# A two-layer diffusion trunk: the last down sweep's weights summed by accumulating DMAs, another order of the down sweeps, and a new plan of the second attention

## The chip, the cores and the metric

The kernel runs on one core of one Trainium2 chip. That core has five engines with instruction streams of their own: TensorE (PE in the profile, with the weight loads listed as PEld), VectorE (DVE), ScalarE (ACT), GpSimd (POOL) and SyncE (SP, which here only issues DMAs). Each executes its stream in order; they wait for one another by semaphores. SBUF is the on-chip memory of 128 partitions, PSUM the memory into which TensorE writes its products.

The metric is the time of one execution on the device in microseconds (us), the median of three runs.

## The reference

A stream of 1024 latent tokens and 256 context tokens, 1024 wide, goes through two layers. Layer 0 mixes tokens by neighbourhood attention, layer 1 by sliding-window attention (radius 128) with 16 query heads over 4 key heads, rotary positions and a sink logit per head. Both layers end with a gated feed-forward part with a convolution of width 3. Context tokens are carried through layer 0 and are only read in layer 1.

```python
for i in range(2):
    sh1, sc1, gt1, sh2, sc2, gt2 = split(silu(c) @ w_mod[i] + b_mod[i])        # the same for the context
    h = rmsnorm(x, g_attn[i]) * (1 + sc1) + sh1
    q, k, v = h @ w_in, q and k normalised per head (rotary in layer 1)
    x = x + gt1 * (attend(q, [k, k_c], [v, v_c]) @ w_out)
    h = rmsnorm(x, g_ffn[i]) * (1 + sc2) + sh2
    u = conv3(h @ w_up) + b;  a, g = halves(u)                                # 2 x 2816 wide
    x = x + gt2 * ((a * silu(g)) @ w_down)
```

Everything is float32 within a tolerance, so the kernel splits each operand of a product into a high and a low part (`whi`/`wlo`, `ghi`/`glo`, `h1hi`/`h1lo`) and runs three matmuls: high by high, high by low, low by high.

## The kernel before

**Stages.** Attention of layer 0, feed-forward of layer 0 (`ffn(0, ...)`), attention of layer 1 (the code that fills the scheduler with `plan_ctx_kv`, `plan_norm`, `plan_sw_qkv` and others, called "the second attention" below), feed-forward of layer 1. Activations lie transposed: 8 blocks `k` of 128 features, and the 1024 tokens in two chunks `c` of 512. The stages that the change touches each have a scheduler `Sched`: operations are declared with an engine, a planned duration, dependencies, a key (rank) and buffers, `run` places them one after the other in planned time, and each engine's instructions are then emitted in that order and stay in it (`InOrder`). `RANKS` holds small corrections of the keys by the number of the operation, one table for each stage. Constants tell a stage what the stage before leaves behind: `LAG` (how long after TensorE each engine is still busy with it), `NREADY` (when the sum of squares for a norm is ready), `LANDED` and `STORED` (when certain transfers are done).

**The down projection.** `a * silu(g)` has 2816 features in 22 blocks, taken as 11 pairs (`NP`). One level of a Strassen-like scheme over token chunks and feature halves makes seven products out of eight. They run in five sweeps over the 11 pairs, `plan_pair(si, i)`; sweeps 0 and 1 make two products each (24 matmuls a pair), sweeps 2, 3 and 4 one (12 matmuls a pair). For each pair SP loads the weights `wraw` and the activations `graw` (from `g_dram`, where the up projection stored them, some as differences made in `block`/`t2`); ACT makes `whi` and `ghi`, DVE makes `wlo` and `glo`, and TensorE adds into four accumulators (`dn`, one of 128 features each) of group a, b, c or d. Some weights are sums: `s3(i)` keeps a difference of two weight blocks in SBUF from sweep 0 on (tiles `s` for the first 8 pairs, `s3lo` for the last 3); sweep 1 replaces it by another combination, and sweeps 3 and 4 each load a weight block and combine it with `s3(i)` on DVE (`wraw<-wraw,s` and `wraw<-wraw,s3lo`) before `whi` and `wlo` can be made.

At the end of a sweep the finished accumulators are added to the residual `xn(c, k)` on DVE (`plan_ev`, in the profile `xn<-dn,modc,xn`), and the results go to `x_dram` (`plan_xd`). In layer 0 the order is 0, 1, 2, 3, 4. Chunk 0 is complete after sweep 2, chunk 1's blocks 0 to 7 after sweep 4, whose accumulators d go into both halves: eight evictions at the end.

**The hand-over to the second attention.** `plan_next` prepares it within the last two sweeps. For chunk 0: sum of squares, reciprocal root (DVE `n1v`, a power on POOL `n1y`, three small DVE steps of a Newton iteration `n1t`, `n1t`, `n1y`, then four DVE copies of a scaled identity `nsum<-idr,n1y`, which TensorE spreads over the partitions as `bc`), then per block a product (`xn<-xn,modc,nsum`) and the split `h1hi`/`h1lo`. For chunk 1 only the squares (ACT `sq`) and their sum (DVE `sums`) are made there. The weights of the context's keys and values (`ckv`) are loaded and split at the end. TensorE then starts the second attention with the context's keys and values (`mm<-whi,h1chi`), goes on with the projections of chunk 0 (`mm<-whi,h1hi`, 24 matmuls of 384 columns for one group of heads and 128 tokens), and needs chunk 1 next: `plan_norm` reduces `sums` (`pt<-invd,sums`), runs the same chain (`n1v`, `n1y`, `S<-idr,n1y`, on TensorE `s<-S,ones`), makes `t<-x,modc,s` on DVE, `h1hi` on ACT and `n1lo` on DVE or POOL. In between, q and k of each 128 tokens are normalised and rotated (`qv`, `qy`, `qn`, `qa`, `qb`, `st`, `klt` on DVE, POOL and ACT) and transposed on TensorE (`pt<-idr,st`, `pt<-idr,klt`).

All of these run through the helper at line 51, so the profile's groups are told apart by tiles, not by lines.

Of the kernel before, what the change touches and what calls it, by code (L numbers as in the profile page):

```python
# [17 lines left out]
P = 128  # L18
D = 1024
KT = 8  # L20
# [18 lines left out]
class InOrder:  # L39
# [7 lines left out]
    def __getattr__(self, name):  # L47
        f = getattr(self.eng, name)

        def call(*a, **k):  # L50
# [25 lines left out]
    ffn0={321: 16.4, 346: 3.3, 364: -15.4, 382: 3.9, 387: 4, 388: -8.1, 389: -5.4, 433: -24.5, 499: 13.3, 502: 17,  # L76
          503: -8.5, 519: 1.9, 548: 28.3, 571: 47.3, 1150: -18.3, 3223: -3.9, 3317: 2.1, 3398: 3.9, 3445: -3.9,
          3455: 9.6, 3469: 6.9, 3609: 20, 3613: 6.8},
    sw={6: -33, 8: -15, 11: 29.2, 14: 18.5, 67: -2.8, 73: -2.8, 74: 57.2, 141: -74.9, 152: 3.4, 162: 17.4, 168:
# [189 lines left out]
def trunk_kernel(ctx, tc, xperm, xtok, xseq, cc, wmod0, wmod, bmod, gnorm, na_wqkv, na_gq, na_gk, na_bias, na_wo,  # L269
# [472 lines left out]
    def plan_norm(sc, l, psa, wk, sums, x, hl, key):  # L742
# [68 lines left out]
        for k in range(KT):  # L811
# [342 lines left out]
    NREADY = 9.2  # L1154
# [279 lines left out]
    def ffn(l, opj, xt1, todo):  # L1434
# [582 lines left out]
        def plan_u(pos, ft, key, C, T):  # L2017
# [55 lines left out]
            sc.op(*LO[512], lambda e: sub(e, YP["t", i][1], V[0][:, :512], YP["t", i][0]), reads=[v, gt + (2,)],  # L2073
# [26 lines left out]
        SWEEPS = (0, 1, 3, 4, 2) if last else (0, 1, 2, 3, 4)  # L2100
# [32 lines left out]
        def plan_pair(si, i):  # L2133
# [10 lines left out]
            def loadg(e):  # L2144
# [6 lines left out]
            sc.op("dma", 1.8 if n > 512 else 1.0, loadw, writes=[I + ("r",)], key=k0 - 14,  # L2151
                  acq=[("raw", I + ("r",), 2 if si == 2 else 3)])
# [7 lines left out]
            elif si == 1:  # L2160
                sc.op(*LO[512], lambda e: sub(e, s3(i), lo_h(), s3(i)), reads=[r_tok], writes=[s_tok], key=k0 - 9, rel=[r_tok])
                src = ((lambda: s3(i), s_tok), (lo_h, r_tok))
            elif si == 2:
                src = ((lo_h, r_tok),)
            else:
                sc.op(*LO[512], lambda e: ENG[e].tensor_tensor(out=lo_h(), in0=lo_h(), in1=s3(i), op=(ALU.subtract, ALU.add)[si - 3]),
                      reads=[s_tok], writes=[r_tok], key=k0 - 9, rel=[r_tok])
                src = ((lo_h, r_tok),)
# [25 lines left out]
            for q in range(nq):  # L2194
                d, starts = prods[q]
                for m in range(4):
                    def mm(e, q=q, m=m, d=d, starts=starts):
# [3 lines left out]
                        for k, (w, g) in enumerate(((0, 0), (0, 1), (1, 0))):  # L2201
# [3 lines left out]
                          writes=[("dn", d, m)], key=k0 + 2.72 * q + (1.36 * m - 2.72 * (i - NP + 2) if si == SWEEPS[-1] and i >= NP - 2 else 0),  # L2205
# [19 lines left out]
        for si in SWEEPS:  # L2225
# [51 lines left out]
    def plan_next(sc, KS, xn, bank, x_tile, plan_sums, plan_bc, plan_t, plan_hilo, u_done, gp, D_):  # L2277
# [50 lines left out]
        for j in range(2):  # L2328
            def load(e, j=j):
# [7 lines left out]
             (lambda k: KS[2] + 5 * (k - 4) if k > 3 else KS[3] - 2 + k, KS[3] + 2, lambda k: KS[3] + 10 + 4 * k),  # L2337
# [7 lines left out]
        for n, k in enumerate(k + 4 * i for k in range(4) for i in range(2)):  # L2345
            ring = ("raw", "sq", "g")[(n % 2 + 1) * (n > 0)]

            def sq(e, k=k, ring=ring):
                if ring == "raw":
                    SQ[k] = sums(e)  # L2350
                elif ring == "sq":
# [4 lines left out]
            sc.op("act", t_act(512), sq, reads=[("xn", 1, k), ("dp",)], writes=[("sq1", k)], key=KS[5], rel=[("xnt", 1, k // 2)],  # L2356
                  acq=[(ring, ("sq1" + ring, k), 1)])

            def add(e, k=k):
                dve.tensor_tensor(out=SQ[0][:, :512], in0=SQ[0][:, :512], in1=SQ[k], op=ALU.add)  # L2360
            if n:
                sc.op("dve", t_dve(512), add, reads=[("sq1", k)], writes=[("sq1", 0)], key=KS[5], rel=[("sq1" + ring, k)])
# [561 lines left out]
```

## Time and profile before

| | us |
|---|---|
| median of three runs (2758.69 to 2758.89) | 2758.88 |
| the profiled execution | 2759.63 |
| its span, first to last instruction | 2757.8 |
| PE busy in the span | 2731.3 |
| DVE, ACT, POOL busy | 2291.1, 1701.8, 418.3 |
| mean granted TensorE clock | 0.999 |

Engine and tile names are those above; `a<-b,c` is an instruction that writes tile a from b and c. In rows of the timeline the first number is the start in us from the span's start, the second the duration of the row's instructions together, `x4` their number, and the bracket at the end the idle time of the engine just before, with what ended it. The times of the profiled execution are used for lengths, the runs for comparisons.

The sweeps of layer 0's down projection lie at about 1423 to 1635 us, the second attention begins there.

### The profile page before, as it was taken

What the parts mean: (1) busy time and instruction counts of PE and PEld (TensorE: products, weight loads), DVE (VectorE), ACT (ScalarE), POOL (GpSimd) and SP (SyncE); (2) the same over time, 40 slices, a digit from 0 to 9 for tenths busy, and PEclk for the clock granted to TensorE, in tenths of its full rate; (3) what the DMA queues carried; (4) which work ended last, traced back from release to release, by engine and by line L of the source; (5) the groups of instructions that cost most, each with busy time, mean ns of one, the idle gap of its engine ahead of it and who ended that gap; (6) DMA issues with size and microseconds to landing.
All of it is one profiled execution on the core that took longest, in us unless ns stands there. A gap on an engine that the chain in (4) does not pass through costs nothing.

```text
span 2757.8 us, 45386 instructions
## 1 busy us (share of the span) xinstructions
PE 2731.3 (99%) x16073; PEld 2431.8 (88%) x16073; DVE 2291.1 (83%) x5005; ACT 1701.8 (62%) x3333; POOL 418.3 (15%) x684
## 2 busy tenths in 40 slices
PE   8999999999999999999999999999999999999999
PEld 7999999999889987788888888999988888888887
DVE  6888878888779678798998698888997989888766
ACT  6877777778556554455554457888874655555443
POOL 1222122223100000000000017546430000000000
PEclk9999999999999999999999999999999999999999
DMA  7222222224745544444476561010254234334745
GB/s 286 80 85 82 73 72 84 91 76 124 263 139 191 184 159 154 153 155 141 159 236 238 172 217 45 14 35 19 77 193 144 73 115 145 123 108 148 256 149 191
DMA packets 144868, 375.60 MB, mean 136 GB/s; under 512 B 22144, under 2 KB 35072, under 8 KB 143232
## 3 DMA queue, kind: packets, MB, share of 16 engines
q1 hardware_dynamic: 144640, 372.70, 40.8%
q8 instruction: 126, 2.06, 0.3%
q14 instruction: 102, 0.84, 0.1%
HBM read 305.59 MB, written 67.04 MB: 135 GB/s over the span
## 4 chain that ended last, share of the span: by engine, by line
PE 70%; DVE 3%; ACT 1%; issue 1%; DMA 0%; POOL 0%; SPq 0%; DVEq 0%; POOLq 0%; ACTq 0%
PE ua L51 17%; PE dn L51 15%; PE uc L51 12%; PE mm L51 6%; PE oacc L51 5%; PE ud L51 4%; PE pt L51 3%; PE pv L51 2%; PE s L51 2%; PE dnc L51 2%; PE u L51 1%; DVE S L51 1%; DVE ptlo L51 0%; PE mod L51 0%; DVE wlo L51 0%
## 5 line engine op out<-in xcount | busy, mean ns | idle before, releaser
L51 ACT ACTIVATE whi<-wraw 128x512 fp32r<-128x512 f32 (+1 forms) x264 | 212.9, 808 | 181.4 <-PE uc L51 55.2
L51 DVE TENSOR_TENSOR wlo<-wraw,whi 128x512 fp32r<-128x512 f32 (+1 forms) x264 | 240.5, 913 | 39.9 <-ACT whi L51 39.4
L51 DVE TENSOR_TENSOR ptlo<-pt,pthi 128x512 fp32r<-128x512 f32 (+2 forms) x384 | 223.0, 596 | 36.1 <-ACT pthi L51 33.8
L51 ACT ACTIVATE S<-S,m 128x640 f32<-128x640 f32 (+3 forms) x288 | 221.2, 770 | 35.8 <-DVE m L51 29.0
L51 PE MATMUL dn<-ghi,whi 128*128 128x512 f32 x616 | 239.9, 390 | 0.0
L51 PE MATMUL dn<-ghi,wlo 128*128 128x512 f32 x616 | 239.7, 389 | 0.0
L51 PE MATMUL dn<-glo,whi 128*128 128x512 f32 x616 | 239.6, 389 | 0.0
L51 ACT ACTIVATE pthi<-pt 128x512 fp32r<-128x512 f32 (+2 forms) x384 | 195.1, 524 | 55.1 <-PE pt L51 35.5
L51 DVE SCALAR_TENSOR_TENSOR u<-c,cv,u 128x1023 f32<-128x1023 f32 x176 | 222.2, 1279 | 3.4 <-ACT u L51 2.9
L51 ACT ACTIVATE whi<-s 128x1024 fp32r<-128x1024 f32 (+1 forms) x116 | 109.0, 940 | 164.0 <-PE uc L51 110.8
L51 ACT ACTIVATE ghi<-graw 128x512 fp32r<-128x512 f32 x154 | 96.4, 630 | 176.4 <-PE dn L51 103.5
L51 PE MATMUL pt<-idr,S 128*128 128x128 f32 x1280 | 195.2, 274 | 2.2 <-DVE qt L51 1.1
L51 PE MATMUL mm<-whi,h0hi 128*128 128x384 f32 x480 | 171.9, 358 | 0.4 <-ACT qraw L51 0.4
L51 DVE TENSOR_TENSOR glo<-graw,ghi 128x512 fp32r<-128x512 f32 x154 | 105.6, 689 | 72.0 <-ACT ghi L51 66.3
L51 PE MATMUL mm<-wlo,h0hi 128*128 128x384 f32 x480 | 162.0, 337 | 0.0
L51 PEld LDWEIGHTS pt<-idr,S 128*128 128x128 f32 x1280 | 149.6, 140 | 10.5 <-DVE ptlo L51 1.9
L51 POOL TENSOR_TENSOR qy<-qv,mhalf 128x4 f32<-128x4 f32 (+1 forms) x112 | 123.2, 1101 | 160.9 <-DVE qv L51 157.5
L51 POOL TENSOR_TENSOR n1y<-n1v,mhalf 128x4 f32<-128x4 f32 (+1 forms) x8 | 8.3, 1041 | 895.3 <-DVE n1v L51 895.3
L51 DVE TENSOR_TENSOR wlo<-s,whi 128x1024 fp32r<-128x1024 f32 (+1 forms) x116 | 124.4, 1075 | 21.3 <-ACT whi L51 21.1
L51 PEld LDWEIGHTS dn<-glo,whi 128*128 128x128 f32 x616 | 115.6, 188 | 24.1
L51 PEld LDWEIGHTS dn<-ghi,whi 128*128 128x128 f32 x616 | 115.6, 188 | 23.9
L51 PEld LDWEIGHTS dn<-ghi,wlo 128*128 128x128 f32 x616 | 115.6, 188 | 23.9
(392 smaller groups left out, 8856.0 us busy)
## 6 DMA issues: line engine op xcount, KB each, us to landing
wraw<-in_w_up_dram SPq DMA_DIRECT2D x132, 512.0 KB, 3.9
wm<-in_wmod_dram SPq DMA_DIRECT2D x80, 512.0 KB, 4.0
wraw<-in_w_down_dram SPq DMA_DIRECT2D x44, 512.0 KB, 3.8
graw<-g_dram SPq DMA_DIRECT2D x44, 512.0 KB, 4.5
wraw<-in_w_down_dram SPq DMA_DIRECT2D x88, 256.0 KB, 3.2
graw<-g_dram SPq DMA_DIRECT2D x66, 256.0 KB, 2.8
slab<-in_na_wqkv_dram SPq DMA_DIRECT2D x32, 384.0 KB, 3.8
woraw<-in_na_wo_dram SPq DMA_DIRECT2D x24, 512.0 KB, 4.5
```

Of the source, the lines that this page charges most:

```text
L51: r = f(*a, **k)
```

## The change

1. In layer 0 the order of the sweeps is 0, 1, 2, 4, 3. So sweep 4 with its accumulators d (eight evictions) is the fourth, and sweep 3, which goes on adding to accumulators a (four evictions, blocks 0 to 3 of chunk 1), the last. Blocks 4 to 7 of chunk 1 are complete one sweep earlier, and are squared and stored then.
2. In layer 0 sweep 3 no longer loads `wraw` by SP and sums on DVE. POOL issues, after sweep 4's own sum has read `s3(i)`, a DMA that adds the weight block from HBM onto `s3(i)` in SBUF (`accum_op=ADD`). Since the DMA can only add, the sign of `s3` is turned round in sweep 1, and that of two stored activations (`t2` and the next) with it. The planner has this as an engine `gq` of its own (3.5 each), with a second token (`sum`, 2.5) until the sum may be read. The scratch space for such DMAs is raised from 64 to 512.
3. `plan_next` squares chunk 1 in the order 4, 5, 6, 7, 0, 1, 2, 3, the first four into a sum of their own during the last sweep. `plan_norm` of layer 1 takes the blocks in the same order, and loads them in it.
4. The constants `LAG`, `LANDED`, `STORED` and `NREADY` are smaller, and `RANKS["ffn0"]` and `RANKS["sw"]` are new, so that both stages are placed anew.

```diff
-    ffn0={321: 16.4, 346: 3.3, 364: -15.4, 382: 3.9, 387: 4, 388: -8.1, 389: -5.4, 433: -24.5, 499: 13.3, 502: 17,
...
+    ffn0={171: 13, 179: 12, 296: -2.6, 297: -15.2, 298: -2.6, 358: 15.1, 387: 12.8, 457: 5.7, 499: 2.7, 542: -1.8,
...
-    LAG = dict(act=5.7, dve=8.9, pool=0.5, dma=10.3)
-    LANDED = (6.9, 10.4)
-    STORED = {0: 2.0, 2: 7.5, 4: 3.0, 6: 10.0}
+    LAG = dict(act=4.2, dve=6.8, pool=0.5, dma=7.9)
+    LANDED = (6.4, 7.9)
+    STORED = {4: 0.3, 6: 0.3, 0: 3.4, 2: 5.2}
...
-        for k in range(KT):
+        for k in range(KT) if l == 0 else (4, 5, 6, 7, 0, 1, 2, 3):
...
-    NREADY = 9.2
+    NREADY = 7.0
...
-                sub(e, YP["t", i][0], V[0][:, 512:], YP[i][1])
+                if last:
+                    sub(e, YP["t", i][0], V[0][:, 512:], YP[i][1])
+                else:
+                    sub(e, YP["t", i][0], YP[i][1], V[0][:, 512:])
...
-        SWEEPS = (0, 1, 3, 4, 2) if last else (0, 1, 2, 3, 4)
+        SWEEPS = (0, 1, 3, 4, 2) if last else (0, 1, 2, 4, 3)
...
-            sc.op("dma", 1.8 if n > 512 else 1.0, loadw, writes=[I + ("r",)], key=k0 - 14,
-                  acq=[("raw", I + ("r",), 2 if si == 2 else 3)])
+            if si == 3 and not last:
+                sc.op("gq", 3.5, lambda e: pool.dma_start(out=s3(i), in_=w_down[l, row][:, c0:c0 + n], accum_op=ALU.add),
+                      reads=[("dw", 4, i, "r")], writes=[("s3p", i)], key=KS[4] + 2.72 * i - 7)
+                sc.op(f"sum{i}", 2.5, lambda e: None, reads=[("s3p", i)], writes=[("s3", i)], key=k0 - 10)
+            else:
+                sc.op("dma", 1.8 if n > 512 else 1.0, loadw, writes=[I + ("r",)], key=k0 - 14,
+                      acq=[("raw", I + ("r",), 2 if si == 2 else 3)])
...
+            elif si == 3 and not last:
+                src = ((lambda: s3(i), s_tok),)
...
                 for m in range(4):
-                    plan_ev("a", m, 1, m, ke + 5)
+                    plan_ev("a", m, 1, m, ke + 5 if last else ke - 20)
+                    if not last:
+                        plan_xd(1, m, ke - 19)
             else:
                 for m in range(4):
-                    plan_ev("d", m, 1, m, ke - 20)
-                    plan_xd(1, m, ke - 19)
+                    plan_ev("d", m, 1, m, ke - 20 if last else ke + 5)
+                    if last:
+                        plan_xd(1, m, ke - 19)
                     plan_ev("d", m, 1, m + 4, ke - 20)
                     plan_xd(1, m + 4, ke - 19)
...
-        for n, k in enumerate(k + 4 * i for k in range(4) for i in range(2)):
-            ring = ("raw", "sq", "g")[(n % 2 + 1) * (n > 0)]
+        for n, k in enumerate((4, 5, 6, 7, 0, 1, 2, 3)):
+            ring = {4: "g2", 0: "raw"}.get(k, ("sq", "g")[n % 2])
+            key = KD + 185 + 5 * n if n < 4 else KS[5]
...
-    nc = _bacc.Bacc("TRN2", target_bir_lowering=False, num_devices=1, dynamic_dma_scratch_size=64)
+    nc = _bacc.Bacc("TRN2", target_bir_lowering=False, num_devices=1, dynamic_dma_scratch_size=512)
```

TensorE's matmuls are the same ones in another order. DVE loses 11 sums of 128x512, SP 11 loads of 256 KB, POOL gains 11 DMAs.

POOL, from the rotary tables (made during sweep 0) to the start of the second attention; `rc` and `rs` are those tables, the first `n1y` belongs to the norm of chunk 0, the second to that of chunk 1. Before:

```order
L51 TENSOR_TENSOR rc<-rc,gqk 128x8x64
L51 TENSOR_TENSOR rs<-rs,gqk 128x8x32 x2
L51 TENSOR_TENSOR n1y<-n1v,mhalf 128x4
L51 TENSOR_TENSOR wlo<-ckv,whi 128x1024 x2
L51 TENSOR_TENSOR vc<-S,vc 128x4x64
```

After:

```order
L51 TENSOR_TENSOR rs<-rs,gqk 128x8x32 x2
L51 DMA s_17484<-in_w_down_dram 128x512 x8
L51 DMA s3lo<-in_w_down_dram 128x512 x3
L51 TENSOR_TENSOR n1y<-n1v,mhalf 128x4
L51 TENSOR_TENSOR wlo<-ckv,whi 128x1024 x2
```

All eleven DMAs stand ahead of the first `n1y`, in one stream with it.

DVE, around the norm of chunk 0. Before (in the fourth sweep; `wraw<-wraw,s` is a sum of weights for it or for the last):

```order
L51 TENSOR_TENSOR wlo<-wraw,whi 128x512
L51 TENSOR_SCALAR n1v<-mp 128x4
L51 TENSOR_TENSOR wraw<-wraw,s_17484 128x512
L51 TENSOR_TENSOR wlo<-wraw,whi 128x512
L51 TENSOR_TENSOR glo<-graw,ghi 128x512
L51 TENSOR_TENSOR wlo<-wraw,whi 128x512
L51 TENSOR_TENSOR wraw<-wraw,s_17484 128x512
L51 TENSOR_TENSOR n1t<-n1y 128x4
L51 SCALAR_TENSOR_TENSOR n1t<-n1t,n1v 128x4
L51 SCALAR_TENSOR_TENSOR n1y<-n1t,n1y 128x4
```

After (at the border of the fourth and the last sweep; `wlo<-s` is a weight split of the last sweep):

```order
L51 TENSOR_TENSOR wlo<-s_17484,whi 128x512
L51 SCALAR_TENSOR_TENSOR xn<-dn,modc,xn 128x512 x5
L51 TENSOR_SCALAR n1v<-mp 128x4
L51 SCALAR_TENSOR_TENSOR xn<-dn,modc,xn 128x512
L51 TENSOR_TENSOR n1t<-n1y 128x4
L51 SCALAR_TENSOR_TENSOR n1t<-n1t,n1v 128x4
L51 SCALAR_TENSOR_TENSOR n1y<-n1t,n1y 128x4
L51 TENSOR_SCALAR nsum<-idr,n1y 128x128 x4
L51 TENSOR_TENSOR wlo<-s_17484,whi 128x512
L51 TENSOR_TENSOR glo<-graw,ghi 128x512 x3
```

The chain of chunk 0's norm has moved from the middle of a sweep to its end, among six of the eight evictions of accumulators d; between `n1v` and `n1t`, where DVE waits for POOL's `n1y`, there is one eviction of cover instead of five instructions. The second split of the last sweep's activations (`glo`) stands behind it.

DVE, from the end of the last sweep to the norm of chunk 1. Before:

```order
L51 SCALAR_TENSOR_TENSOR xn<-dn,modc,xn 128x512 x8
L51 TENSOR_TENSOR wlo<-ckv,whi 128x1024 x2
L51 TENSOR_TENSOR sums_19580<-sums_19580,sq 128x512 x2
L51 TENSOR_TENSOR wlo<-slab,whi 128x768
L51 TENSOR_TENSOR sums_19580<-sums_19580,sq 128x512 x5
L51 TENSOR_REDUCE ckvv<-qsq 128x4
L51 TENSOR_TENSOR wlo<-slab,whi 128x768
L51 TENSOR_SCALAR n1v<-pt 128x4
```

After:

```order
L51 SCALAR_TENSOR_TENSOR xn<-dn,modc,xn 128x512 x3
L51 SCALAR_TENSOR_TENSOR h1lo_19323<-xn,modc,h1hi_19321 128x512
L51 SCALAR_TENSOR_TENSOR xn<-dn,modc,xn 128x512
L51 TENSOR_TENSOR wlo<-ckv,whi 128x1024
L51 TENSOR_TENSOR sq<-sq 128x512
L51 TENSOR_TENSOR wlo<-ckv,whi 128x1024
L51 TENSOR_TENSOR sums_19553<-sums_19553,sq 128x512 x4
L51 TENSOR_TENSOR wlo<-slab,whi 128x768 x2
L51 TENSOR_REDUCE ckvv<-qsq 128x4
L51 TENSOR_TENSOR vc<-S,vc 128x4x64
L51 TENSOR_SCALAR n1v<-pt 128x4
```

Four evictions and two sums of squares fewer stand there. On TensorE the spreading of that norm (`s<-S,ones`) comes after 27 projection matmuls of chunk 0 instead of 48, and the first transposition of rotated keys (`pt<-idr,klt`) after 147 projection matmuls instead of 114, counted from `pt<-invd,sums`, which stands at the same place in both (behind 48 matmuls for the context).

More of the change, by code (lines that the diff above doesn't have):

```diff
@@ L2072, in plan_u @@
             store(1, lambda: YP[i][0], gt + (3,), gt)
-            sc.op(*LO[512], lambda e: sub(e, YP["t", i][1], V[0][:, :512], YP["t", i][0]), reads=[v, gt + (2,)],
+            sc.op(*LO[512], lambda e: ENG[e].tensor_tensor(out=YP["t", i][1], in0=V[0][:, :512], in1=YP["t", i][0],
+                                                           op=ALU.subtract if last else ALU.add), reads=[v, gt + (2,)],
                   writes=[gt + (4,)], key=key - 9, rel=[v])
@@ L2164, in plan_pair @@
                 src = ((lo_h, r_tok),)
+            elif si == 3 and not last:
+                src = ((lambda: s3(i), s_tok),)
             else:
-                sc.op(*LO[512], lambda e: ENG[e].tensor_tensor(out=lo_h(), in0=lo_h(), in1=s3(i), op=(ALU.subtract, ALU.add)[si - 3]),
+                sc.op(*LO[512], lambda e: ENG[e].tensor_tensor(out=lo_h(), in0=lo_h(), in1=s3(i), op=(ALU.add if last and si == 4 else ALU.subtract)),
                       reads=[s_tok], writes=[r_tok], key=k0 - 9, rel=[r_tok])
@@ L2390, in trunk_kernel @@
     gqk, sink, bandt, rc, rs = [C1[n] for n in ("gqk", "sink", "bandt", "rc", "rs")]
-    xs[1] = Parts([lo_part("x1", F32) for _ in range(4)], 2)
+    X1 = [lo_part("x1", F32) for _ in range(4)]
+    xs[1] = Parts(X1[2:] + X1[:2], 2)
     ph = ExitStack()
@@ L2746, in trunk_kernel @@
     table(sc, AF.Exp, lambda: CK["v", 0][:, 0, :1].bitcast(F32), ("ckv", "vh", 0), 5.0)
-    for j in range(0, KT, 2):
+    for j in (4, 6, 0, 2):
         sc.op(f"stored{j}", STORED[j], lambda e: None, writes=[("stored", j)], key=-300)
```

31 lines of the change are left out of this document (18 added, 13 removed), and 30 rows, old and new, of tables (ffn0, sw).

## The prediction

> **What bounds the kernel.** I read the page's busy times first, then TensorE's waits by name in the part that the change touches, then the timeline of TensorE at the longest of them, the stretches around it, and last the other engines' rows there.
>
> ```profile
> PE 2731.3 (99%) x16073; PEld 2431.8 (88%) x16073; DVE 2291.1 (83%) x5005; ACT 1701.8 (62%) x3333; POOL 418.3 (15%) x684
> ```
>
> TensorE is busy for 2731.3 of 2757.8 us. The change removes no matmul, so it can win only where TensorE stands still or is slow: 26.5 us in the whole span. Its waits from the end of the down projection to the end of the second attention (1635 to 2080 us):
>
> ```profile
> PE pt L51 <- ACT st L51: 2.3, 1, 2.3
> PE s L51 <- DVE m L51: 1.2, 1, 1.2
> PE pt L51 <- DVE ptlo L51: 0.8, 3, 0.4
> PE mm L51 <- POOL n1lo L51: 0.6, 1, 0.6
> PE mm L51 <- DVE o0lo L51: 0.6, 1, 0.6
> PE pt L51 <- DVE klt L51: 0.3, 1, 0.3
> PE mm L51 <- ACT whi L51: 0.2, 1, 0.2
> ```
>
> Three of the seven, 2.3 by `st`, 0.3 by `klt` and 0.6 by `n1lo`, lie at one place, the first transposition of rotated keys and what stands behind it:
>
> ```profile
> 1669.82 0.33 PE L51 MATMUL mm<-whi,n1lo 128*128 128x384 f32 x1
> 1670.00 0.34 PE L51 MATMUL mm<-wlo,h1hi 128*128 128x384 f32 x1
> 1672.67 0.28 PE L51 MATMUL pt<-idr,st 128*128 128x128 f32 x1 [2.33 <-ACT st L51]
> 1673.30 0.28 PE L51 MATMUL pt<-idr,klt 128*128 128x128 f32 x1 [0.35 <-DVE klt L51]
> 1673.41 0.41 PE L51 MATMUL mm<-whi,h1hi 128*128 128x384 f32 x1
> 1674.43 0.44 PE L51 MATMUL mm<-whi,n1lo 128*128 128x384 f32 x1 [0.61 <-POOL n1lo L51]
> ```
>
> Starts tell more than modelled ends. A matmul of 384 columns lets the next start 0.18 later (1669.82 to 1670.00), a transposition after 0.11 (1673.30 to 1673.41). So the three places cost 2.67 - 0.18 = 2.49, 0.63 - 0.11 = 0.52 and 1.02 - 0.18 = 0.84, together 3.85 us. The stretches show a second cost:
>
> ```profile
> 1660.00:1670.00 10.00, 10.00 (x60) 9.66 (x58) 10.00 (x25) 7.66 (x15) 6.03 (x7) 1.00 0.01 2
> 1670.00:1680.00 10.00, 6.71 (x35) 5.86 (x35) 5.03 (x11) 4.34 (x12) 10.00 (x13) 0.83 0.00 0
> ...
> 1675.44:1678.85 3.41, 3.41 (x18) 3.31 (x17) 0.93 (x1) 1.95 (x5) 3.41 (x4) 0.50 0.00 0
> ```
>
> The columns are the stretch, then busy PE, PEld, DVE, ACT, POOL, then the granted clock. DVE is full up to the stall (10.00 of 10.00), POOL full through it, and after it TensorE has half its clock for 3.41 us: 3.41 x 0.5 = 1.7 us. The place costs 3.85 + 1.7 = 5.55 us in all. TensorE waits there for a chain on DVE, POOL and ACT that starts when the down projection ends.
>
> **1. The end of the down projection (sweep order, squares, sums).**
>
> ```profile
> 1635.94 0.40 PE L51 MATMUL mm<-whi,h1clo 128*128 128x512 f32 x1
> 1636.17 0.39 PE L51 MATMUL mm<-wlo,h1chi 128*128 128x512 f32 x1
> ...
> 1639.03 1.41 DVE L51 TENSOR_TENSOR sums<-sums,sq 128x512 f32<-128x512 f32 x2
> 1642.53 4.14 DVE L51 TENSOR_TENSOR sums<-sums,sq 128x512 f32<-128x512 f32 x5
> 1647.81 0.16 DVE L51 TENSOR_SCALAR n1v<-pt 128x4 f32<-128x4 f32 x1
> 1651.30 0.87 DVE L51 TENSOR_SCALAR S<-idr,n1y 128x128 f32<-128x128 f32 x4
> 1672.65 0.60 DVE L51 TENSOR_TENSOR klt<-qa,st 128x128 fp32r<-128x128 f32 x1 [1.58 <-ACT st L51]
> ```
>
> After, DVE has there four evictions fewer and, with the add of the two half sums, two adds fewer: an add takes 4.14 / 5 = 0.83 with its gaps, an eviction 7.7 / 11 = 0.70 (row below), so some 4 x 0.70 + 2 x 0.83 = 4.5 us of DVE go from this place into the last sweep. The `n1v` at 1647.81 follows TensorE's `pt<-invd,sums`, which stays behind 48 context matmuls of 512 columns, 0.23 apart (1635.94 to 1636.17), some 11 us; so this chain itself does not start earlier by 4.5 us. What gets earlier is what stood behind: `S` came 3.5 + 0.9 = 4.4 us after `n1v`, `t` and the rotations queued behind it on DVE.
>
> TensorE's side decides more. The first `pt<-idr,klt` has 147 projection matmuls ahead of it instead of 114: 33 x 0.18 = 5.9 us of cover; 0.18 is a rounded distance, and I take 5.7. The keys came 2.49 + 0.52 = 3.0 us too late. With 5.7 us of cover and the same DVE work ahead of them they are 2.7 us early, and more by what DVE was relieved of. `n1lo` is now needed at the 86th instead of the 98th of these matmuls, 2.1 us earlier, but its chain starts with `s<-S,ones` after 27 matmuls instead of 48, 3.8 us earlier. So all three waits go, and with them the half clock: -5.55. I take the 0.2 by `whi` (context weights queued among eight squares, now among four) as gone too. Of the 1.2 by `m`, in a stretch that the new plan orders otherwise, I take half: -0.6. The other waits, 0.8 and 0.6, I leave as they are. Sum of gains: -6.35.
>
> Costs at the same place: `S` is ready 4.4 us after `n1v`, and TensorE has 27 x 0.18 = 4.9 us of work in that time. The margin is 0.5 us; I put a wait of 0.2 for it, between 0 and 1.
>
> **2. The last two sweeps.**
>
> ```profile
> 1574.00:1605.00 31.00, 31.00 (x146) 25.92 (x145) 29.55 (x54) 17.24 (x29) 1.39 (x1) 1.00 0.65 203
> 1605.00:1635.00 30.00, 30.00 (x134) 24.83 (x133) 27.24 (x44) 16.38 (x26) 3.72 (x2) 1.00 0.64 198
> ...
> L51 DVE TENSOR_TENSOR glo<-graw,ghi 128x512 fp32r<-128x512 f32 x21 | 14.3, 688 | 0.5 <-ACT ghi L51 0.3
> L51 DVE TENSOR_TENSOR wlo<-wraw,whi 128x512 fp32r<-128x512 f32 x20 | 13.6, 686 | 0.1
> L51 DVE SCALAR_TENSOR_TENSOR xn<-dn,modc,xn 128x512 f32<-128x512 f32 x11 | 7.7, 747 | 2.5 <-PE dn L51 2.5
> L51 DVE SCALAR_TENSOR_TENSOR xn<-xn,modc,nsum 128x512 f32<-128x512 f32 x8 | 5.9, 746 | 0.1
> L51 DVE SCALAR_TENSOR_TENSOR h1lo<-xn,modc,h1hi 128x512 fp32r<-128x512 f32 x8 | 5.9, 746 | 0.0
> ...
> L51 DVE TENSOR_TENSOR wraw<-wraw,s x16: 681/685/693, 1563.3 to 1620.1; 128x512 f32<-128x512 f32 x16
> 1619.53 0.69 DVE L51 TENSOR_TENSOR wlo<-wraw,whi 128x512 fp32r<-128x512 f32 x1
> 1620.13 0.69 DVE L51 TENSOR_TENSOR wraw<-wraw,s 128x512 f32<-128x512 f32 x1
> ...
> 1582.22 1.39 POOL L51 TENSOR_TENSOR n1y<-n1v,mhalf 128x4 f32<-128x4 f32 x1 [130.17 <-DVE n1v L51]
> 1675.78 1.73 POOL L51 TENSOR_TENSOR n1lo<-t,h1hi 128x512 fp32r<-128x512 f32 x1
> ...
> wraw<-in_w_down_dram SPq DMA_DIRECT2D x88, 256.0 KB, 3.2
> ```
>
> The two stretches are about the fourth and the fifth sweep; the groups are those of 1574 to 1635. TensorE never stands there, so the 11 sums taken from DVE (11 x 0.685 = 7.5 us) and the 11 loads taken from SP win nothing by themselves: TensorE's full 30 us a sweep covers them. They make room for what comes in. Row by row, the last sweep asks of DVE eight evictions of d and four of a (12 x 0.70 = 8.4), 11 `wlo` and 11 `glo` (22 x 0.69 = 15.2), eight products and eight splits of chunk 0 (16 x 0.746 = 11.9), some 3 us for the norm's chain and two adds: 38.5 us. Starts lie closer than busy times (1619.53 to 1620.13: 0.60 for a 0.69); at that ratio it is nearer 35. The sweep has 30, splits run ahead into the sweep before, and the last four evictions fall behind it. It fits, with little left.
>
> The tight place is the border, where DVE holds five evictions, `n1v`, one eviction, the wait for `n1y`, three Newton steps, `nsum`, and only then `glo`. That is 6 x 0.70 + 1.39 + 0.9 + 0.9, some 7.4 us, in which TensorE has two pairs (24 matmuls of 0.23, 5.5 us) and what `glo` is ahead by. So it may wait between 0 (two pairs ahead) and 2 us (7.4 - 5.5); of the ends I am nearer the lower one, since before too TensorE met eight evictions in a row without a wait: +0.55.
>
> **The DMAs on POOL.** No row shows a DMA issued by POOL, nor one that adds. What it holds POOL for, g, lies between nothing much (SP's issues do not count as busy) and the landing of a load as on SP plus a POOL pass, 3.2 + 1.3 = 4.5 us; with the memory read and written twice some 5.8. (1.3 is the shorter `n1lo` on POOL, 1.73 the longer.) Transfers have time: each is wanted a sweep, 30 us, after the sum that releases it. The queue behind is what can cost. POOL is idle 130 us ahead of `n1y`, but after the change that `n1y` stands behind all 11. The first can go at 1563.3 + 0.7 = 1564.0; `n1v` comes at about 1604.8, at the border. (1604.8 - 1564.0) / 11 = 3.7 us a DMA is the point up to which nobody waits; above it each 0.1 costs DVE, and all the splits behind `n1t`, 1.1 us. I take g as 1.3 to 3, nearest to a POOL pass of that shape: cost 0. At g = 4.5 it is (4.5 - 3.7) x 11 = +8.8 us.
>
> The Trainium skill, "DMA: Bandwidth & Descriptors", section "Anatomy of one DMA — SWDGE (gpsimd) path", prices such a DMA at 2.0 us plus its bytes over 436 GB/s; by that, 256 KB make an estimated 2.6 us, and the sum would stay as it is. A rule against the change is in "SBUF — State Buffer", the box "DVE blocks DMA": while DVE runs in its two-port mode, it holds the port that GpSimd needs to write descriptors, so that a DMA issued there starves. No run here has shown it yet; POOL's 1.39 us for `n1y` beside a DVE busy 29.55 of 31 us speaks against a general lockout. By it the eleven issues would each wait for gaps; the fourth rival prices that from rows.
>
> **Sum.** -5.55 (first transposition) - 0.2 (`whi`) - 0.6 (`m`) + 0.2 (`s<-S,ones`) + 0.55 (border) = -5.6 us. The new plan of the second attention beyond that I cost at nothing: its other waits, 0.8 and 0.6, are all there is to win, and as much may come anew; the bounds are -1.4 and, by the largest wait of that stage, +2.3. The profiled execution took 2759.63, 0.75 above the median of the runs; it gives 2754.0, and the median 2753.3. A measurement of this kernel can tell about 0.2% (5.5 us) from no change, so "faster" ends at 2753.4 and "slower" begins at 2764.4.
>
> **The rivals.**
>
> - *All waits of the second attention go.* If the plan also hides 0.8 + 0.6 + the other 0.6 by `m` and the border costs nothing, another 2.6 us go: some 2750.7. For it: DVE, POOL and ACT are no bound there over the whole stage. Against: three different engines release those waits.
> - *The gain is given back.* DVE, with 35 of the last sweep's 30 us and its border, stalls TensorE 2 us at the border and 1 to 2 at the end, or a new wait like that of 2.3 comes up in the new plan: 2753.3 + 3.5 = 2757. For it: 29.55 and 27.24 of 31 and 30 already, and eight evictions moved there; against: 7.5 us of sums are gone.
> - *POOL's issues are slower than 3.7 us each* (the other side). Then `n1y` comes late, DVE stands at `n1t`, `glo` behind it, and TensorE runs dry at the border. At 4.5 us it is 2753.3 + 8.8 = 2762, with a half clock after such a wait as above (1.7) 2764; it eats the whole gain 5.6 / 11 = 0.5 us above 3.7, at g = 4.2, and is slower by 0.2% at (5.6 + 5.5) / 11 = 1.0 above, at 4.7, or 4.55 with the half clock. For it: the planner gives each 3.5, close to the threshold; against: nothing is known that makes the issue wait for the landing.
> - *DVE locks POOL's issues out.* DVE is idle 1.45 of 31 us. If each of 11 issues lost one POOL pass of 1.3 to that, they would end 14.3 us later: unnoticed up to a pace of 3.7 - 1.3 = 2.4 without it, and with all of it 2753.3 + 14.3 = 2767.6 at a pace of 3.7. Against it speaks the `n1y` of 1.39.
> - *The keys still come late*, because the chain of chunk 1's norm is not shorter: then only the cover counts, 5.7 against 3.0 us. It would need 2.7 us of new work on DVE ahead of `klt`; the time would be 2757 to 2759.
>
> **How the numbers follow.** The forecast as summed, from 2 us below to 2 above, has 0.45; all waits go 0.18; the gain given back, with late keys, 0.22; POOL's issues 0.10; the lockout 0.05. The range from 2749.0 to 2761.0 takes in the first three cases with the bounds (low end: the second case's 2750.7 less another 1.7, should a second stretch of half clock go with its waits; high end: the third case's 2757 with a new wait of 2.3 and its half clock of 1.7) and leaves out the last two. Faster by over 0.2%: the second case and a little over half of the first, whose border term may be 0: 0.18 + 0.25 = 0.43. Within 0.2%: the rest of the first, 0.20, the third but for 0.02, and 0.02 of POOL's with g near 4: 0.42. Slower: 0.08 of POOL's, the lockout, and 0.02 of the third, should late keys meet a border of 2 us and a new wait: 0.15.
>
> **What would show it.** Right: no wait by `st` near 1670, clock 1.00 in that stretch; TensorE without idle time at the border (near 1605) and in the last sweep; POOL's `n1y` within 2 us of `n1v`. Wrong: the 11 issues more than 3.7 us apart, `n1y` late and `n1t` on DVE waiting for POOL; `glo` or `bc` as what ends TensorE's waits before 1635; a wait at `s<-S,ones`, or another one of over 1 us with a half clock behind it later in the second attention.

## The result and the profile after

The changed kernel takes 2779.77 us (median of four runs, 2779.01 to 2782.85) against 2758.89 for the kernel before: a ratio of 1.0076, 95% interval 1.0062 to 1.0091. It is 21 us slower. The profiled execution is the longest of the four, 2782.85 us with a span of 2781.1.

The engines' busy times, from the page after; TensorE's matmuls are as many as before, but it is busy 11 us longer:

```profile
PE 2742.6 (99%) x16073; PEld 2435.1 (88%) x16073; DVE 2282.9 (82%) x4987; ACT 1701.2 (61%) x3334; POOL 431.8 (16%) x701
```

TensorE's waits after, from the fourth sweep to the end of the second attention (1560 to 2110 us; engine, what ended the wait, us in total, times, longest):

```profile
PE bc L51 <- DVE nsum L51: 8.6, 1, 8.6
PE dn L51 <- DVE glo L51: 3.6, 2, 3.3
PE mm L51 <- ACT qraw L51: 1.5, 1, 1.5
PE pt L51 <- DVE st L51: 1.2, 1, 1.2
PE pv L51 <- ACT pthi L51: 1.1, 2, 1.0
...
PE pv L51 <- DVE ptlo L51: 0.9, 1, 0.9
```

The waits of before by ACT `st`, by `klt`, by `n1lo` and by `whi` are gone, as forecast, and that by `m`, of which half was forecast to go. The six others shown have come. The largest is at the border of the last two sweeps, where POOL and DVE read so after (start, duration, idle time before it):

```profile
1565.16 1.06 POOL L51 DMA_DIRECT2D s<-in_w_down_dram  x1 [113.47 <-ACT ghi L51]
...
1602.00 0.88 POOL L51 DMA_DIRECT2D s<-in_w_down_dram  x1 [3.85 <-ACT whi L51]
1607.12 0.88 POOL L51 DMA_DIRECT2D s3lo<-in_w_down_dram  x1 [4.24 <-ACT sq L51]
1612.30 0.89 POOL L51 DMA_DIRECT2D s3lo<-in_w_down_dram  x1 [4.30 <-ACT whi L51]
1616.38 0.89 POOL L51 DMA_DIRECT2D s3lo<-in_w_down_dram  x1 [3.18 <-issue]
1616.96 1.36 POOL L51 TENSOR_TENSOR n1y<-n1v,mhalf 128x4 f32<-128x4 f32 x1
...
1607.17 0.15 DVE L51 TENSOR_SCALAR n1v<-mp 128x4 f32<-128x4 f32 x1
1618.36 0.16 DVE L51 TENSOR_TENSOR n1t<-n1y 128x4 f32<-128x4 f32 x1 [10.38 <-POOL n1y L51]
```

An issue keeps POOL busy for 0.88 us only, but the eleven start 5.12 us apart on average, (1616.38 - 1565.16) / 10, with 4.0 to 6.2 from one to the next, whatever the idle rows name as releaser. `n1y` is wanted at 1607.3, but stands behind all of them and starts at 1616.96. DVE idles 10.38 us, TensorE 8.6 at `bc`, and it comes back with half its clock (0.71 and 0.89 in the rows below). At the end of the last sweep DVE is held up in another way, and at the start of the second attention there is a stall again:

```profile
1642.34 0.68 DVE L51 TENSOR_TENSOR wlo<-s3lo,whi 128x512 fp32r<-128x512 f32 x1
1642.94 2.92 DVE L51 SCALAR_TENSOR_TENSOR xn<-xn,modc,nsum 128x512 f32<-128x512 f32 x1
1645.79 2.83 DVE L51 TENSOR_TENSOR glo<-graw,ghi 128x512 fp32r<-128x512 f32 x1
...
1642.77 5.29 POOL L51 TENSOR_TENSOR wlo<-ckv,whi 128x1024 fp32r<-128x1024 f32 x2 [24.45 <-ACT whi L51]
...
1612.00:1620.00 8.00, 0.71 (x3) 0.71 (x4) 1.54 (x8) 0.00 (x0) 2.83 (x3) 0.71 0.43 66
1620.00:1630.00 10.00, 10.00 (x44) 8.39 (x44) 10.00 (x17) 5.50 (x10) 0.00 (x0) 0.89 0.35 107
1680.00:1690.00 10.00, 7.28 (x32) 6.99 (x31) 7.23 (x22) 6.76 (x15) 6.57 (x6) 0.68 0.01 2
```

While POOL makes its two splits of context weights, DVE's operations beside them take 2.92 and 2.83 us instead of the 0.74 and 0.69 that the same ones take elsewhere. The last `glo` is late by that: 3.3 us of TensorE.

From the first down matmul to the last, the down projection of layer 0 is 19.7 us longer than before (1422.79 to 1654.05 against 1423.44 to 1635.01), the second attention, from `pt<-invd,sums` to its last output product, 1.6 us longer. And the down projection of layer 1, whose code is unchanged, is 2.95 us longer without a single wait. The same 100 us of it hold 443 matmuls before and 436 after (busy PE with its count, PEld, DVE, ACT, clock 1.00 in both). Before:

```profile
2580.00:2680.00 100.00, 100.00 (x443) 82.81 (x442) 8.22 (x12) 2.72 (x4) 1.00 0.58 187
```

After:

```profile
2580.00:2680.00 100.00, 100.00 (x436) 81.40 (x435) 5.36 (x8) 0.00 (x0) 1.00 0.57 197
```

Its matmuls start 0.2299 us apart there on average, instead of 0.2267.

### The profile page after: what moved, and what is told of

Its sections match the earlier page's. It is cut to its first block, busy times and chain, and to the rows that moved or that the text cites. A ratio compares the mean times of both kernels' runs of the same rounds, so it can differ in the third digit from the quotient of the medians.

```text
span 2781.1 us, 45409 instructions
## 1 busy us (share of the span) xinstructions
PE 2742.6 (99%) x16073; PEld 2435.1 (88%) x16073; DVE 2282.9 (82%) x4987; ACT 1701.2 (61%) x3334; POOL 431.8 (16%) x701
## 4 chain that ended last, share of the span: by engine, by line
PE 91%; DVE 3%; issue 2%; DMA 2%; ACT 1%; POOL 1%; SPq 0%; POOLq 0%; DVEq 0%; ACTq 0%
PE mm L51 18%; PE ua L51 17%; PE dn L51 13%; PE uc L51 13%; PE pt L51 7%; PE pv L51 5%; PE s L51 5%; PE oacc L51 5%; PE ud L51 4%; PE dnc L51 2%; PE u L51 1%; DMA tok<-in_xtok_dram 1%; DMA x<-in_xperm_dram 0%; DVE S L51 0%; PE mod L51 0%
## 5 line engine op out<-in xcount | busy, mean ns | idle before, releaser
L51 ACT ACTIVATE whi<-wraw 128x1024 fp32r<-128x1024 f32 (+1 forms) x253 | 206.4, 816 | 182.5 <-PE uc L51 52.5
L51 DVE TENSOR_TENSOR wlo<-wraw,whi 128x1024 fp32r<-128x1024 f32 (+1 forms) x253 | 232.8, 922 | 39.1 <-ACT whi L51 38.9
L51 PE MATMUL uc<-t34h,whi 128*128 128x512 f32 x336 | 131.2, 391 | 0.0
```

Source lines behind the costliest of these rows:

```text
L51: r = f(*a, **k)
```

## The experiments

The first theory (A) for POOL's pace: the descriptor space that was raised to 512 bytes holds one such DMA, so that each issue waits for the landing of the one before. For it speaks that in the packet records of the trace each issue follows the last packet of the DMA before by 0.60 to 0.68 us, all ten times. The rivals are a lockout by DVE (B) and a fixed price of an adding DMA (C).

**More room for descriptors.** SBUF is full, so room is made by storing a padded vector compactly.

```diff
-    cpad = cpool.tile([P, KT, 32], F32, name="cpad")
+    cpad = cpool.tile([P, 48], F32, name="cpad")
...
-    nc = _bacc.Bacc("TRN2", target_bir_lowering=False, num_devices=1, dynamic_dma_scratch_size=512)
+    nc = _bacc.Bacc("TRN2", target_bir_lowering=False, num_devices=1, dynamic_dma_scratch_size=1024)
```

> The changed kernel with 1024 bytes of descriptor space a partition for POOL's DMAs instead of 512 (the padded conditioning vector at the start of the program is stored in 48 columns instead of 256 to make room; its other columns are read by no result). Theory A, the space holds the descriptors of one such DMA, and the next issue waits until the one before has landed: now at least two are under way at once, the issues follow the sums of the fourth sweep (2.5 to 3 us apart on average, instead of 5.1), n1y starts within 2 us of n1v, and TensorE's waits of 8.6 us at bc and 3.6 at glo go with their half clock; time 2760 to 2766. Theory B, DVE's use of the port shared with POOL holds the issues up: more space changes nothing, issues stay 4 to 6 us apart, time 2777 to 2782. Theory C, a DMA that adds costs POOL about 5 us whatever the space: as B.

2773.94 us, ratio 1.0056 (1.0039 to 1.0073). POOL with 1024 bytes:

```profile
1593.07 0.88 POOL L51 DMA_DIRECT2D s<-in_w_down_dram  x1 [3.13 <-ACT whi L51]
1596.05 0.88 POOL L51 DMA_DIRECT2D s3lo<-in_w_down_dram  x1 [2.10 <-DVE glo L51]
1598.45 0.88 POOL L51 DMA_DIRECT2D s3lo<-in_w_down_dram  x1 [1.52 <-DVE glo L51]
1602.55 0.88 POOL L51 DMA_DIRECT2D s3lo<-in_w_down_dram  x1 [3.23 <-issue]
1609.21 1.03 POOL L51 TENSOR_TENSOR n1y<-n1v,mhalf 128x4 f32<-128x4 f32 x1 [5.79 <-DVE n1v L51]
```

The issues now follow the sums, down to 2.4 us apart, and POOL waits for `n1v` instead of the other way round. The wait at `bc` is gone. Theory A holds, B and C fall: between 1590 and 1605 DVE is busy for 8.7 of 15 us here, with the issues 2.4 to 4.1 us apart, while after the change it idled between 1608 and 1618 and the issues still came 5.18 and 4.08 us apart. But the time fell by 6 us, not by the 14 to 20 expected; the waits at `glo` stayed (4.1 us), and the matmuls of both down projections were slower still (4.5 us in layer 1's).

> The changed kernel with 576 bytes of descriptor space instead of 512. Theory A with 9 packets of each of two sides for each of 16 engines (1584 packets in 11 DMAs are 144 each), 16 bytes each: 576 bytes hold 36, just two DMAs, and then the issues come closer than 4 us, and the time falls to about that of 1024 bytes. If one place must stay free, or a DMA needs more, two don't fit and the issues stay at 5.1 us, time 2777 to 2783. Theories B and C: no change.

One run, 2766.1 us. The issues come 2.4 to 4.2 us apart with one gap of 7.3, where a sum was late: 64 bytes more are enough for two DMAs at once. And its matmuls go at 0.2267 us again. So 512 bytes cost twice.

**`n1y` ahead of the last three DMAs.** One number of the planner; on POOL it moves `n1y`, and nothing else moves on any engine.

```diff
-                sc.op("gq", 3.5, lambda e: pool.dma_start(out=s3(i), in_=w_down[l, row][:, c0:c0 + n], accum_op=ALU.add),
+                sc.op("gq", 5.2, lambda e: pool.dma_start(out=s3(i), in_=w_down[l, row][:, c0:c0 + n], accum_op=ALU.add),
```

> The changed kernel with one number of the planner altered, a POOL DMA of this kind planned at 5.2 us instead of 3.5. The one thing that this moves is POOL's n1y for chunk 0, from behind all 11 DMAs to ahead of the last three; the space stays at 512. Theory A and the theory that the whole loss at the border is n1y's place in POOL's queue: issues stay about 5.1 us apart, but n1y starts within 2 us of n1v, the wait at bc goes, and the time falls by 12 to 17 us to 2762 to 2768. If DVE is late at the border for another reason (six evictions in a row), the wait at bc stays above 3 us and the time above 2772.

2769.01 us, ratio 1.0035 (1.0022 to 1.0048):

```profile
1601.46 0.88 POOL L51 DMA_DIRECT2D s<-in_w_down_dram  x1 [3.71 <-issue]
1603.68 1.03 POOL L51 TENSOR_TENSOR n1y<-n1v,mhalf 128x4 f32<-128x4 f32 x1 [1.33 <-DVE n1v L51]
1605.70 0.92 POOL L51 DMA_DIRECT2D s3lo<-in_w_down_dram  x1 [0.99 <-issue]
1610.16 0.88 POOL L51 DMA_DIRECT2D s3lo<-in_w_down_dram  x1 [3.53 <-ACT whi L51]
```

The DMAs are as slow as before, TensorE doesn't wait at `bc`, and 10.8 us are gone: the place of one 1 us operation in POOL's queue. Expected were 12 to 17.

**The sums back on DVE, in the new order.**

```diff
-            if si == 3 and not last:
-                sc.op("gq", 3.5, lambda e: pool.dma_start(out=s3(i), in_=w_down[l, row][:, c0:c0 + n], accum_op=ALU.add),
...
-            else:
-                sc.op("dma", 1.8 if n > 512 else 1.0, loadw, writes=[I + ("r",)], key=k0 - 14,
-                      acq=[("raw", I + ("r",), 2 if si == 2 else 3)])
+            sc.op("dma", 1.8 if n > 512 else 1.0, loadw, writes=[I + ("r",)], key=k0 - 14,
+                  acq=[("raw", I + ("r",), 2 if si == 2 else 3)])
```

> The changed kernel without its accumulating DMAs: the last sweep's 11 weights are loaded by SP and summed on DVE as before the change; the new sweep order, squares and second attention stay. If the DMAs are the whole loss and the order and the plan win what was forecast: 2752 to 2758, below the kernel before. If the new order or plan loses by itself (a new wait of the second attention takes the place of the 2.3 us one): 2759 to 2765. If the 11 sums on DVE are what the new order can't carry: TensorE waits for glo or wlo in the last sweep, above 2765.

2769.41 us, ratio 1.0036 (1.0023 to 1.0049), the third case's range, but not for its reason. TensorE's waits for DVE in the sweeps:

```profile
PE dn L51 <- DVE glo L51: 1.1, 2, 0.7
PE dn L51 <- DVE wlo L51: 0.6, 1, 0.6
```

That is 1.7 us, and 5.9 us (2 x 2.95) are the pace of the matmuls, since the 512 bytes were left in. Without these it would stand at an estimated 2763.5, the second case: the new order and plan lose by themselves, without any accumulating DMA. In its trace the second attention is 5.0 us longer than before the change.

**Where the tiles lie.** Theory D: the 512 bytes at the bottom of SBUF move all tiles above them by 448 bytes, and with that the matmuls' pace.

```diff
-    nc = _bacc.Bacc("TRN2", target_bir_lowering=False, num_devices=1, dynamic_dma_scratch_size=64)
+    nc = _bacc.Bacc("TRN2", target_bir_lowering=False, num_devices=1, dynamic_dma_scratch_size=512)
```

> The kernel before with 512 bytes of descriptor space instead of 64 and nothing else: no DMA uses it, but all tiles at lower addresses of SBUF lie 448 bytes further up. Theory D, the matmuls of both down projections go at 0.2300 instead of 0.2267 us apart in the runs with 512 and 1024 bytes (and not with 576) because of where the weights and activations lie: the same here, 2 x 2.95 us, so 2764 to 2766. Rival, that pace comes from the accumulating DMAs or from the state of the chip: 2758 to 2760 and 0.2267.

2764.30 us, ratio 1.0018 (1.0009 to 1.0028): 5.2 us for space that nothing uses. The same stretch of layer 1's down projection in this kernel:

```profile
2580.00:2680.00 100.00, 100.00 (x435) 81.47 (x434) 8.23 (x12) 2.73 (x4) 1.00 0.58 188
```

The counterpart puts the tiles of the changed kernel 64 bytes further up, with the descriptor space left at 512:

```diff
+    cpool.tile([P, 16], F32, name="pad")
     cpad = cpool.tile([P, KT, 32], F32, name="cpad")
```

> The changed kernel with an unused tile of 64 bytes a partition ahead of the others, so that its tiles lie where they lie with 576 bytes, while the space for descriptors stays 512. Theory D: the down projections' matmuls go at 0.2267 us again, 5.9 us less, 2772 to 2775; the issues of POOL's DMAs stay 5.1 us apart and the wait at bc stays above 7 us. Rival (576 was faster because of its descriptors alone): 2778 to 2781.

```profile
2580.00:2680.00 100.00, 100.00 (x443) 82.81 (x442) 5.36 (x8) 0.00 (x0) 1.00 0.59 200
...
PE bc L51 <- DVE nsum L51: 11.4, 1, 11.4
```

The pace is back, the DMAs stay 4 to 6.7 us apart, but the time is 2777.78 us (ratio 1.0071, 1.0056 to 1.0087), 2 us less and not 5.9. The second row, from TensorE's waits, says why: layer 1's half is won, but in layer 0 POOL's queue sets the time of `n1y`, TensorE only comes to the border earlier and waits 11.4 us there instead of 8.6. Theory D holds; its price in layer 0 depends on what else bounds the stage. With 576 bytes the tiles lie where they lie here, and its one run is 11.7 us faster: this is the price of POOL's queue with no tile moved. By the edits, the tiles lie further up than in the kernel before by 512 bytes in these two, whose pace is the same, and by 448 (512 bytes of space) or 128 (1024 bytes and the compact vector) in the slow ones. Which relation of addresses counts was not settled.

**POOL's splits beside DVE.** From here on with 576 bytes.

```diff
-            sc.op(*(("pool", 2.28) if i < 2 else ("dve", t_dve(1024) + 0.03)), lo, reads=[("slr", i), ("slh", i)], writes=[("sll", i)],
+            sc.op("dve", t_dve(1024) + 0.03, lo, reads=[("slr", i), ("slh", i)], writes=[("sll", i)],
```

> The changed kernel with 576 bytes, and the two splits of context weights that POOL makes at the end of the last sweep put on DVE. Theory E, each of these splits holds DVE's operation beside it up by 2.1 us (2.9 and 2.8 instead of 0.7), the last glo comes late by that, and TensorE's wait of 3.4 us with 1.7 of half clock follows from it: both go, and 2 x 1.1 us more on DVE are hidden; 2766 - 5 = 2761 (2759 to 2763). Rival, DVE is simply full at the end of the last sweep: with more work on it the wait stays or grows, 2765 to 2769.

2762.54 us, ratio 1.0014 (1.0005 to 1.0024); 3.6 us less than the one run with 576 bytes. The ten runs of the new kernel spread over 4.8 us, so this size is rough. TensorE's waits for `glo` (1560 to 2110 us) with 576 bytes and the splits on POOL:

```profile
PE dn L51 <- DVE glo L51: 5.0, 4, 3.4
```

With the splits on DVE:

```profile
PE mm L51 <- ACT qraw L51: 1.5, 1, 1.5
PE pt L51 <- DVE st L51: 1.3, 2, 1.2
...
PE dn L51 <- DVE glo L51: 0.8, 2, 0.5
```

The wait of 3.4 us is gone with 2.3 us more work on DVE: theory E holds, DVE was held up, not full. Half the clock did not follow that wait with 576 bytes (the granted clock is 1.00 until 1670), so the 1.7 us expected for it were not there to win.

**The second attention.** The forecast said that the new plan wins 5.5 us; in the traces the second attention is as long as before. First the numbers of the kernel before:

```diff
-    LAG = dict(act=4.2, dve=6.8, pool=0.5, dma=7.9)
-    LANDED = (6.4, 7.9)
+    LAG = dict(act=5.7, dve=8.9, pool=0.5, dma=10.3)
+    LANDED = (6.9, 10.4)
...
-    NREADY = 7.0
+    NREADY = 9.2
```

with `RANKS["sw"]` of before.

> The changed kernel with 576 bytes, and the second attention's numbers (RANKS, LAG, LANDED, NREADY) of the kernel before. The forecast's claim that the new plan wins 5.5 us: it is lost here, 2770 to 2773. Theory F, the new plan has only moved the stall from the rotated keys to the context's keys (1.2 by st, 1.5 by qraw and their half clock of 3.4): about the same time, 2764 to 2768.

2787.67 us, ratio 1.0105 (1.0090 to 1.0120), 21 us above the same kernel with its own numbers. Both theories missed by far. New waits are spread over the whole stage, the largest sum 4.8 us:

```profile
PE pt L51 <- DVE ptlo L51: 4.8, 8, 2.3
```
 The tables fit one hand-over each, so this run says nothing on the worth of the new plan.

Then the stall itself. Four operations are moved at the end of the planner's `run`:

```diff
+        if n == 3091:
+            for i, j, d in ((160, 71, 0), (129, 71, 0), (38, 186, 1), (39, 38, 1)):
+                order.remove(i)
+                order.insert(order.index(j) + d, i)
         self.end, self.free = end, free
```

> The kernel r576_ckvdve with four operations moved at the start of the second attention, nothing else: on ScalarE the two evacuations qraw<-mm stand ahead of a norm product and of two evacuations of the context's keys, and on TensorE the last of the four transpositions of the context's keys comes 12 projections later. Theory G: the stall of the new plan there (1.2 us by st, 1.5 us by qraw, half clock behind them, 6.1 us in all against 5.4 in the kernel before) is these two queues, not a lack of work; both waits and most of the half clock go, 2762.5 - 4 to - 5, so 2757 to 2759, about the kernel before or just below. Rival: the norm of chunk 1 is late by itself and TensorE waits for it next (h1hi or n1lo, within 3 us): 2761 to 2763.

2758.27 us, ratio 0.9998 (0.9989 to 1.0007). TensorE's waits from 1640 us on have 0.2 by `qraw` and 0.2 by `st`, and the clock stays up. The stretch before the move, in r576_ckvdve, and after it:

```profile
1667.00:1677.00 10.00, 9.04 (x37) 9.04 (x38) 3.89 (x17) 3.98 (x11) 7.47 (x10) 0.67 0.01 2
```

```profile
1670.00:1680.00 10.00, 10.00 (x61) 9.97 (x60) 7.89 (x28) 6.36 (x17) 9.03 (x12) 1.00 0.00 0
...
PE mm L51 <- ACT qraw L51: 0.2, 1, 0.2
PE pt L51 <- DVE st L51: 0.2, 1, 0.2
```

61 matmuls in 10 us instead of 37, at full clock. Theory G holds: 4.3 us, most of the 5.55 that were forecast for this place, lay behind two queues that the change had made anew. From `pt<-invd,sums` to the last output product it is now 4.1 us shorter than in the kernel before.

**What the accumulating DMAs are worth.** The same kernel with the sums on DVE (the edit of dvesum) and 64 bytes:

> The kernel qraw_first with the last sweep's weights loaded by SP and summed on DVE instead of by the accumulating DMAs, and 64 bytes of descriptor space as in the kernel before; order of sweeps, squares, splits and second attention as there. If DMAs with room for two at once are worth anything (11 sums of 0.69 us less on DVE), this one is slower by 2 to 8 us, TensorE waiting for glo or wlo in the last sweep. If the sums were covered by TensorE anyway, it is the same within 1.5 us; if the DMAs cost more by delaying SP's loads of the fourth sweep (landing after 4.7 us instead of 3.0) than they save, it is faster by 1 to 2 us.

2758.79 us, ratio 0.9999 (0.9991 to 1.0008): no difference that can be measured. And with every second sum by a DMA:

```diff
-            if si == 3 and not last:
+            by_dma = si == 3 and not last and i % 2 == 1
+            if by_dma:
```

> The kernel qraw_first with only every second sum of the last sweep (5 of 11) made by an accumulating DMA, the other six loaded by SP and summed on DVE. Theory H: with all 11 by DMA the loads of the fourth sweep land late (TensorE loses 2 to 6 us there on glo), with all 11 on DVE the last sweep is too full (3 us); half of each loses less than either, 2754.5 to 2757, faster than the kernel before. Rival: both losses come with the sweep order and not with the sums' place: 2758 to 2760, no difference.

2758.76 us, ratio 0.9999 (0.9990 to 1.0008). Theory H falls, and the time is the rival's: the three ways cost the same. That the losses come with the order of the sweeps, as the rival has it, isn't shown; no run puts the mended second attention behind the old order. SP's loads of weights in the fourth sweep land after 3.0 us in the kernel before (median), and beside eleven accumulating DMAs after 5.4 (4.3 to 5.1 in the other traces with eleven):

```profile
DMA to landing us min/median/max: 2.7/3.0/4.1
```

```profile
DMA to landing us min/median/max: 3.0/5.4/7.9
```

The first row is of the kernel before, the second of qraw_first. In their profiled executions, from the first down matmul of layer 0 to the last, qraw_first, dvesum_fix and half_dma are 6.5, 4.1 and 5.3 us longer than the kernel before, in waits for `glo` and `wlo`; that takes what the second attention won (4.1, 3.6 and 4.5). They lose at different places: the fourth sweep takes 37.4, 31.1 and 34.9 us, the last 30.6, 34.5 and 31.8, against 31.8 and 29.7 before. But such a length is one execution's: r576_ckvdve, in which all engines do the same up to there as in qraw_first, is only 2.6 us longer than the kernel before, its fourth sweep 33.5. No version here is faster than the kernel before.

## Why the prediction was wrong, step by step

- **The step that failed first: "I take g as 1.3 to 3, nearest to a POOL pass of that shape: cost 0."** Measured 5.12 us. The upper bound beside it, 4.5 if an issue waits for the landing, was the mechanism, and its row (a load on SP lands after 3.2) was too short; the 5.8 beside it was above the measured pace. The adding DMAs, median us to landing in the last column:

```profile
s<-in_w_down_dram POOLq DMA_DIRECT2D x8, 256.0 KB, 5.0
s3lo<-in_w_down_dram POOLq DMA_DIRECT2D x3, 256.0 KB, 4.0
```

The rival "POOL's issues are slower than 3.7 us each" happened just as described, with a chance of 0.10. It rests on one queue: 10.8 us by the move of `n1y`.
- **The rest of the loss was not in that rival's price.** At its 4.5 it stood at 2762 to 2764. At the measured pace its rule gives (5.12 - 3.7) x 11 = 15.6 us, so 2769. But from the first issue to the last there are ten steps and not eleven, and the last holds POOL for 0.9 us only: `n1y` came 9.6 us late, and the move of it won 10.8. The queue alone would have made the forecast some 2764, by estimate (2753.3 + 10.8); the rest is in the next three points, whose sizes need not add up.
- **The raised descriptor space was costed at nothing; it isn't in the prediction at all.** 5.2 us in the kernel before, by the pace of matmuls that the change doesn't touch. No row of before shows it, but an edit that moves every tile's address is one to bound.
- **"It fits, with little left" for DVE in the last sweep** looked at DVE's own work. Before, POOL's two splits lie beside DVE's evictions and 1.90 us of idle time:

```profile
1629.54 2.40 POOL L51 TENSOR_TENSOR wlo<-ckv,whi 128x1024 fp32r<-128x1024 f32 x1 [45.93 <-ACT whi L51]
1630.68 2.77 DVE L51 SCALAR_TENSOR_TENSOR xn<-dn,modc,xn 128x512 f32<-128x512 f32 x4 [1.90 <-PE dn L51]
1633.68 2.40 POOL L51 TENSOR_TENSOR wlo<-ckv,whi 128x1024 fp32r<-128x1024 f32 x1 [1.74 <-ACT whi L51]
```

Nothing in the prediction asked what would lie beside them after. It cost some 3.6 us.
- **"So all three waits go, and with them the half clock: -5.55."** They went. But the context's keys, whose transpositions stand after 63 to 72 projections in the new order (48 to 60 before), and the `qraw` evacuations behind them came late: waits of 1.5 and 1.2 us and 6.8 us of half clock, some 6.1 us, as much again. The prediction asked of `n1lo` and of `S` whether they would be late next, not of the transpositions ahead of `klt`. When their queues were put right, 4.3 us came. The rival "The gain is given back", with 0.22, had named such a new wait, and a stall of 1 to 2 us at the end of the last sweep, where one of 3.3 came.
- **Right:** the 11 sums taken from DVE win nothing by themselves; `s<-S,ones` without a wait; the border without a wait as soon as `n1y` is in time (forecast 0.55); transfers of the sums in time.
- **"Transfers have time"** was true of the sums and false of their neighbours: SP's loads beside them landed later.
- **The lockout of POOL's issues by DVE**, which the Trainium skill, "SBUF — State Buffer", box "DVE blocks DMA", describes for DVE's two-port mode, didn't show; whether DVE's operations beside the issues run in that mode no run here shows. An issue took 0.88 or 0.89 us with DVE idle (1612.30 above) and with DVE at work (the rows of ring1024). What showed is the other direction, DVE slowed by POOL's operations.
- The estimate of 2.6 us by the Trainium skill, "DMA: Bandwidth & Descriptors", section "Anatomy of one DMA — SWDGE (gpsimd) path", is below the 4.0 and 5.0 us measured for an adding DMA of 256 KB beside SP's loads in this stage; the measurement decides.

From the changed kernel down, by medians but for the one run with 576 bytes: 2779.8, with 576 bytes 2766.1 (queue and placement together, 13.7), without POOL's splits 2762.5 (3.6), with the second attention's queues put right 2758.3 (4.3).

## What to carry to other kernels

Before DMAs are put on POOL, ask how many fit into the descriptor space at once, and what stands behind them in POOL's queue: a full space turns every issue into a wait for a landing, and the price is paid by the next short operation of a chain. Price a buffer at the bottom of SBUF also by the addresses it moves, and read the distance of matmuls' starts in stages the change doesn't touch. When a plan removes a stall, look in the new order for the next transposition or evacuation at that place, and see which engine's queue holds it.

## What the runs showed of the hardware that was not expected

- An accumulating DMA of 128 rows of 2 KB: with 512 bytes a partition of descriptor space the next one is issued 0.60 to 0.68 us after the last packet of the one before; with 576 two are under way at once.
- The pace of matmuls 128x128 by 128x512 in the down projections depends on where tiles lie: on average 0.2267 us from start to start with descriptor spaces of 64 and 576 bytes (or 512 and 64 of padding), 0.2299 with 512, 0.2316 in the kernel with 1024, at a granted clock of 1.00 in all. The matmuls of the up projection didn't change.
- A POOL split of 128x1024 on two SBUF operands stretches a DVE operation of 128x512 on two SBUF operands beside it from 0.7 to 2.8 or 2.9 us. In the six traces with such pairs, the DVE operation ends 0.55 or 0.56 us after the split beside it (1645.86 and 1645.31 after the change). DVE's evictions, which read a PSUM tile, kept their 0.74 to 0.75 us beside the same splits before.
- In the wait of 8.6 us after the change, TensorE's granted clock fell to half 4.6 us after the wait began, for 6.8 us, of which 2.9 lay behind the wait. Single waits of 3.1 to 3.4 us for `glo` went with half clock for 3.4 us (after the change, gq52, ring1024), for 6.8 (pad64) or not at all (576 bytes, half_dma).
